# A state-space layer inside an attention phase: one generator per unit cut into a front and a back with step tables of their own

## The chip, the cores and the metric

The kernel runs on one core of a Trainium2 chip. The metric is the device time of one execution in microseconds (us), taken as the median of several executions. The engines are called PE (TensorE, the matrix multiplies; PEld is its weight load), ACT (ScalarE), DVE (VectorE), POOL (GpSimd) and SP (SyncE, which here only issues DMAs; SPq is its queue).

## The reference

One layer of a trunk with two parallel head groups, for 2048 tokens of width 1024, all in float32. The part that the change touches is the state-space mixer: 32 groups of 16 channels, each group with one diagonal complex state of 64 entries.

```python
h = rmsnorm(x, norm_mix_g)
proj = h @ w_in                      # u_ssm | q | k | v, 512 columns each
# head group A: S5 layer
bu = einsum('bsgh,gph->bsgp', u, b_bar)          # 16 inputs -> 64 complex states
_, states = associative_scan(combine, (lam_bar, bu), axis=1)
y = einsum('bsgp,ghp->bsgh', states, c_mat).real + d_skip * u
y = gelu(y.reshape(bsz, seq, 512))
y_ssm = y * sigmoid(y @ w_glu + b_glu)
# head group B: 64-frame chunks that see themselves and the 8 chunks before
y_att = chunked_attention(q, k, v, attn_rel_bias)
mixed = concat([rmsnorm(y_ssm), rmsnorm(y_att)])
x = x + mixed @ w_out
x = x + (silu(rmsnorm(x) @ w_gate) * (rmsnorm(x) @ w_up)) @ w_down
out = rmsnorm(x)
```

## The kernel before

Products of float32 accuracy are made of three passes over operands that are split into a high and a low part (names that end in h and l, or begin with hi and lo). TensorE's instructions are pinned in the order in which the program issues them; the other engines' order follows from a scheduler with those pins.

The kernel has phases: projection of the first block, the attention phase, the mixing phase (GELU, GLU, output projection), and the feed-forward network. The state-space layer is computed inside the **attention phase** (`att_phase`). That phase goes through 128 steps, one for each token block sb (4 blocks of 512 tokens), head pair pr (4), head of the pair hh (2) and query tile qp (4). In each step, in the order of `ORDER = "sptf"`, come the scores of the step (tile `sc`; VectorE adds the bias at L857, ScalarE takes the exponential at L860), the product of probabilities and values of a head that is complete, the transposes of the probabilities of two steps ago (tile `pt`; ScalarE's cast `pth` at L875, VectorE's remainder `ptl` at L876), and last the filler units.

A filler is a generator in a `Unit`: its yields are spread evenly over the steps s0 to s1, and its first piece may be taken `pre` steps ahead. Fillers are the projections of the next block (tile `pf`), queries, keys and values, and the eight units of the state-space layer, b = 0 to 7, each with four of the 32 groups (`GB` = 4). `SU` gives the steps between which each unit lies: 2, 19, 35, 49, 64, 78, 93, 107 and 122.

A unit works on chunks of eight tokens, so that the scan runs over 256 chunks (`NC`) rather than over 2048 tokens. It has these parts, in `ssm_unit`:

- loads on SyncE's queue at L564: the input `U` (eight DMAs), `Bst` (one), `Tm` (eight) and `Vm` (one), then `YL` = 8 empty sub-steps;
- the front product U times Bst into the PSUM tile `pj`, which ScalarE copies into `X` (L588, eight copies);
- the scan over the chunks on GpSimd (L602 to L614), on X in place;
- the shifted states `XG`, written from X by four DMAs on GpSimd's queue (L636), then `YX` = 9 empty sub-steps;
- the back product Tm times U plus Vm times XG into `pj`, copied by ScalarE (L646) into a tile `Y` that takes X's buffer, and stored by eight DMAs on SyncE's queue (L649) to the buffer `y` in device memory.

That makes 42 sub-steps over 13 to 17 steps. U, X, XG, Tm, Vm and Bst have one buffer each, so a unit's loads wait until the unit before has read them, and its copies into X until the unit before has stored Y.

The mixing phase opens at step `OPEN` = 119: it asks for the GLU weights (`load_wg`, raw tile `sg`, cast at L156 into `wgh` and `wgl`) and then, in `load`, for the first two blocks of y (tile `yr`, L1031). Its GELU stands at L1035 (tile `ys`), its casts into `gh` at L156, and the first GLU product `pf<-gh,wgh` follows at step 122 and later (`GSTART`). The attention's last steps run beside it.

`S["rsn"]` is an SBUF tile of 2048 columns, one per token, that holds the roots of the RMS norms. The first norm's are read when a block's input is scaled (tile `hT`, for block 1 at about steps 20 to 26, for blocks 2 and 3 later); the feed-forward norm's are written over them from the mixing phase on. Its first half, for blocks 0 and 1, is thus unused in between.

Of the kernel before, what the change touches and what calls it, by code (L numbers as in the profile page):

```python
# [16 lines left out]
P = 128  # L17
# [3 lines left out]
NG, CH, NS = 32, 16, 64  # L21
NPR = NG // 2
L = 8
NC = SEQ // L
GB, GP = 4, 2
# [20 lines left out]
SL = 1  # L46
LPH = 2
V0 = 0, 4
DB, XB = 3, 2
SU = 2, 19, 35, 49, 64, 78, 93, 107, 122  # L50
CUT = -8, -2, 2, 7, 13, 19, 24
CUTL = -8, -2, 2, 7, 13, 19, 23
ORDER = "sptf"
PINA = True
YL = 8
YX = 9
X1B = 6
TAIL = (0, 512), (512, 256), (768, 256)
MAGIC = 12582912.0
# [494 lines left out]
    return nb  # L554


def ssm_unit(k, p, psum, S, b, eng):

    nc = k.nc
    F = GB * CH  # L560
    U = k.t(p, "U", [P, GB, NC])

    def load(out, in_):
        ins = nc.sync.dma_start(out, in_)  # L564
# [5 lines left out]
    gs = slice(GB * b, GB * b + GB)  # L570
    bst = k.t(p, "Bst", [P, GB, P])
    load(bst[:].rearrange("p g m -> p (g m)"), S["bst"][b // 2][:, (b % 2) * GB * P : (b % 2 + 1) * GB * P])
    tm = k.t(p, "Tm", [P, GB, P])
    for i in range(L):
        load(tm[i * CH : (i + 1) * CH], S["kt"].rearrange("c g a m -> c g (a m)")[:, gs, P - CH * i : 2 * P - CH * i])
    vm = k.t(p, "Vm", [P, GB, P])
    load(vm[:], S["v"].rearrange("q g c n m -> (c n) (q g) m")[:, gs, CH:])
    for _ in range(YL):
        yield

    X = k.t(p, "X", [P, 2, GP, NC])
    for q in range(GP):
# [51 lines left out]
    for g2 in range(2):  # L634
        for c in range(2):
            eng.dma_start(XGv[c * NS : (c + 1) * NS, :, g2, 1:], X[g2 * NS : (g2 + 1) * NS, c, :, : NC - 1])  # L636
# [16 lines left out]
SSM_N = YL + GP + 7 + 7 + 3 + 4  + YX + GP  # L653


class Unit:
# [21 lines left out]
def att_phase(k, ident, S, aw, x0, roots):  # L678

    tc, nc, io, pfs = k.tc, k.nc, k.io, k.pfs  # L680
    with ExitStack() as cx:
# [253 lines left out]
        for sb in range(NSB):  # L935
            g0 = sb * 32
            C = CUT if sb < NSB - 1 else CUTL
            if sb > 0:
                if DB:
                    units.append(Unit(hT_unit(sb, 0, DB), 2 + DB, g0 + HTA[0], g0 + HTA[1], 2))  # L940
                units += [Unit(hT_unit(sb, DB), 2 + KT - DB, g0 + HTS[0], g0 + HTS[1], HTP), Unit(qk_unit(sb, 0), QK_N, g0 + C[0], g0 + C[1], 3, light=LIGHT)]
            units.append(Unit(v_unit(sb, 0), V_N, g0 + C[1], g0 + C[2], 2, light=LIGHT) if sb else Unit(v0, V_N, *V0, done=1))
            for gen, n, c in ((qk_unit(sb, 1), QK_N, 2), (qk_unit(sb, 2), QK_N, 3), (v_unit(sb, 1), V_N, 4), (qk_unit(sb, 3), QK_N, 5)):
                units.append(Unit(gen, n, g0 + C[c], g0 + C[c + 1], 2, light=LIGHT) if sb else Unit(gen, n + 1, C[c], C[c + 1], 4, light=LIGHT, mid=2))
        for b in range(NG // GB):
# [28 lines left out]
def mix_phase(k, S, bank):  # L974
# [3 lines left out]
    with ExitStack() as cx:  # L978
# [41 lines left out]

        yrs = [None]

        def load(sb, one=False):
            b = B()
            b.o = {}
            yt = k.t(my, "ys", [P, 4, SB], bufs=2)
            b.ys, b.g = [yt[:, f] for f in range(4)], []
            if sb % 2 == 0:
                yrs[0] = k.t(my, "yr", [P, 4, L, 128])
                for f in range(4):  # L1030
                    nc.sync.dma_start(yrs[0][:, f], S["y"][f * P : (f + 1) * P, :, sb * 64 : sb * 64 + 128])  # L1031
            yv = b.yr = yrs[0][:, :, :, (sb % 2) * 64 : (sb % 2 + 1) * 64]
            fs = [slice(0, 4)] if one else [slice(f, f + 1) for f in range(4)]
            for s in fs:
                nc.scalar.activation(yt[:, s].rearrange("p f (c j) -> p f c j", j=L), yv[:, s].rearrange("p f j c -> p f c j"), AF.Gelu_apprx_tanh)  # L1035
# [100 lines left out]
        def pre_tiles():  # L1136
            while True:
# [579 lines left out]
```

## Time and profile before

| | |
|---|---|
| median of 3 executions | 2294.59 us (2293.13 to 2301.24) |
| profiled execution | 2293.41 us, span of its trace 2291.6 us |
| mean granted clock of TensorE | 0.978 |
| TensorE busy | 2172.1 us, 95% of the span |
| VectorE, ScalarE, GpSimd busy | 1542.1, 1000.9, 359.2 us |
| the window 128 to 752 us (attention phase) | TensorE busy 551.0 of 624 us, granted clock 0.95 |
| the window 752 to 985 us (mixing phase) | TensorE busy 224.3 of 233 us, granted clock 0.98 |
| DMA | 428.34 MB moved, mean 187 GB/s |

In the profile's rows an operation reads "output<-inputs", with the line in the kernel ahead of it (L79 and L82 are the helpers that record every matmul and transpose, so products are told apart by their tiles). An "x8" behind a row counts neighbouring instructions of one kind. What stands in square brackets behind a row of the timeline is the engine's idle time ahead of it and what ended that.

### The profile page before, as it was taken

How to read it: one execution, taken by the hardware profiler on the slowest of the kernel's cores; microseconds unless marked ns; L12 is line 12 of the kernel's file. 1: busy time of each engine (PE TensorE's matmuls, PEld its weight loads, DVE VectorE, ACT ScalarE, POOL GpSimd, SP SyncE). 2: the span in 40 equal slices, each digit the busy share in tenths (PEclk: the TensorE clock that was granted, in tenths of full speed). 3: DMA queues.
4: the chain of work that ended last, by engine and by line, in shares of the span. 5: the costliest groups of instructions: out<-in, count | busy, mean ns of one | idle time of the engine just before them, and what ended most of it. 6: DMA issues, size and time to landing. Idle time of an engine off the chain costs nothing.

```text
span 2291.6 us, 30320 instructions
## 1 busy us (share of the span) xinstructions
PE 2172.1 (95%) x10632; PEld 1828.7 (80%) x10632; DVE 1542.1 (67%) x2695; ACT 1000.9 (44%) x1654; POOL 359.2 (16%) x827
## 2 busy tenths in 40 slices
PE   8987799989987899999999999999999999999997
PEld 6776688888986688878888887888888878888886
DVE  7745565555545855876776668666656477788776
ACT  6445555455546652343333335333333343354322
POOL 2246645456641000000000000000000010000000
PEclk9999999999998999999999999999999999999999
DMA  8766777766644434854564557564423295465552
GB/s 292 241 219 225 227 236 193 190 181 191 191 120 143 161 111 146 284 176 145 162 200 165 198 184 261 184 198 161 167 87 121 84 397 196 165 212 193 207 188 74
DMA packets 214872, 428.34 MB, mean 187 GB/s; under 512 B 38848, under 2 KB 61424, under 8 KB 207616
## 3 DMA queue, kind: packets, MB, share of 16 engines
q1 hardware_dynamic: 207072, 401.49, 54.2%
q0 software_dynamic: 7648, 24.92, 3.2%
q8 instruction: 83, 1.36, 0.2%
q14 instruction: 69, 0.57, 0.1%
HBM read 286.86 MB, written 129.00 MB: 181 GB/s over the span
## 4 chain that ended last, share of the span: by engine, by line
PE 73%; POOL 8%; issue 6%; DVE 4%; DMA 3%; ACT 2%; SPq 1%; DVEq 0%; POOLq 0%; ACTq 0%
PE X L79 20%; PE ps L79 17%; PE Y L79 10%; PE big L79 9%; PE pf L79 5%; PE W L79 5%; PE pj L79 3%; POOL X L605 2%; POOL st L602 1%; POOL st L603 1%; POOL X L604 1%; POOL X L614 1%; POOL fx L613 1%; PE sc L79 1%; PE pt L82 1%
## 5 line engine op out<-in xcount | busy, mean ns | idle before, releaser
L79 PE MATMUL X<-hi,c 128*128 128x512 f32 x1408 | 451.6, 391 | 7.7 <-DVE c L156 5.4
L79 PE MATMUL ps<-hd,hd 128*128 128x512 f32 (+1 forms) x1968 | 428.2, 379 | 3.2 <-DVE hd L156 2.0
L79 PEld LDWEIGHTS ps<-hd,hd 128*128 128x128 f32 x1968 | 356.4, 188 | 73.4 <-DVE hd L156 2.7
L79 PEld LDWEIGHTS X<-hi,c 128*128 128x128 f32 x1408 | 265.6, 189 | 64.0 <-DVE c L156 6.3
L79 PE MATMUL X<-lo,c 128*128 128x512 f32 x704 | 275.1, 391 | 0.0
L156 ACT CAST hd<-hd 128x1536 fp32r<-128x1536 f32 (+1 forms) x106 | 147.3, 1394 | 232.8 <-DMA hd<-hq 165.5
L79 PE MATMUL Y<-hi,c 128*128 128x512 f32 x704 | 225.1, 390 | 1.9 <-DVE u L1396 1.9
L156 DVE TENSOR_TENSOR hd<-hd 128x1536 fp32r<-128x1536 f32 (+1 forms) x106 | 174.1, 1644 | 35.0 <-ACT hd L156 34.5
L156 DVE TENSOR_TENSOR c<-S,c 128x512 fp32r<-128x512 f32 x176 | 121.0, 688 | 100.6 <-ACT c L156 100.3
L1500 POOL DMA_DIRECT2D hd<-hq x7 | 5.3, 764 | 1133.4 <-PE X L79 1121.1
L1392 ACT COPY u<-X 128x512 f32<-128x512 f32 x132 | 77.5, 588 | 201.4 <-PE X L79 201.4
L156 ACT CAST c<-S 128x512 fp32r<-128x512 f32 x176 | 109.4, 622 | 119.8 <-PE Y L79 61.6
L79 PE MATMUL big<-m,woh 128*128 128x512 f32 x512 | 161.0, 396 | 0.0
L1534 DVE TENSOR_TENSOR acc<-acc,ps 128x512 f32<-128x512 f32 x196 | 130.4, 683 | 41.6 <-PE ps L79 41.4
L79 PEld LDWEIGHTS Y<-hi,c 128*128 128x128 f32 x704 | 132.8, 189 | 30.5 <-DVE u L1396 2.8
L79 PEld LDWEIGHTS X<-lo,c 128*128 128x128 f32 x704 | 132.9, 189 | 27.7
L79 PE MATMUL pf<-hi,w 128*128 128x512 f32 x416 | 150.1, 412 | 4.0 <-ACT hi L736 4.0
L156 ACT CAST c<-raw 128x512 fp32r<-128x512 f32 x132 | 82.3, 623 | 151.4 <-PE Y L79 68.5
L79 PE MATMUL Y<-lo,c 128*128 128x512 f32 x352 | 137.3, 390 | 0.0
L876 DVE TENSOR_TENSOR ptl<-pt,pth 128x640 fp32r<-128x640 f32 (+3 forms) x152 | 98.3, 647 | 45.9 <-ACT pth L875 44.4
L860 ACT ACTIVATE s<-s,mn 128x640 f32<-128x640 f32 (+4 forms) x128 | 98.0, 765 | 58.5 <-DVE mn L857 53.6
L875 ACT CAST pth<-pt 128x640 fp32r<-128x640 f32 (+3 forms) x152 | 83.8, 551 | 87.4 <-PE pt L82 82.5
(443 smaller groups left out, 4290.3 us busy)
## 6 DMA issues: line engine op xcount, KB each, us to landing
w<-wss SPq DMA_DIRECT2D x36, 1024.0 KB, 6.3
hq<-g SPq DMA_DIRECT2D x140, 256.0 KB, 2.1
hd<-hq SPq DMA_DIRECT2D x35, 768.0 KB, 4.4
hd<-wc SPq DMA_DIRECT2D x35, 768.0 KB, 5.9
raw<-in_w_gate SPq DMA_DIRECT2D x44, 512.0 KB, 3.7
raw<-in_w_up SPq DMA_DIRECT2D x44, 512.0 KB, 4.2
wc<-px SPq DMA_DIRECT2D x66, 256.0 KB, 3.4
wss<-w SPq DMA_DIRECT2D x12, 1024.0 KB, 4.9
```

The costliest lines, as they stand in the source:

```text
L79: return self.tc.keep_in_program_order(self.tc.nc.tensor.matmul(*a, **b))
L82: return self.tc.keep_in_program_order(self.tc.nc.tensor.transpose(*a, **b))
L156: return nc.scalar.copy(hi, raw), nc.vector.tensor_tensor(lo, raw, f32(hi), op=ALU.subtract)
L602: eng.tensor_tensor(t[:, :, :, :n], src, ar, op=ALU.mult)
L603: eng.tensor_tensor(t2[:, :, :, :n], src[:, ::-1], aw, op=ALU.mult)
L604: eng.tensor_tensor(dst, dst, t[:, :, :, :n], op=ALU.add)
L605: eng.tensor_tensor(dst, dst, t2[:, :, :, :n], op=ALU.add)
L860: nc.scalar.activation(s[:, :nk], s[:, :nk], AF.Exp, bias=mn[:], scale=-1.0, accum_out=sums[sb, pr][:, hh, qp : qp + 1])
L875: nc.scalar.copy(pth[:, a:b, qp, :], pt[:, a:b, :])
L876: nc.vector.tensor_tensor(ptl[:, a:b, qp, :], pt[:, a:b, :], f32(pth[:, a:b, qp, :]), op=ALU.subtract)
L1392: nc.scalar.copy(u[:], ps[:])
L1534: V.tensor_tensor(a, a, ps[:], op=ALU.add)
```

## The change

`ssm_unit` is cut in two generators. `ssm_front` has the loads of U and Bst, the front product, the scan and the XG DMAs, in 25 sub-steps over nine steps from `SX[b]` on (4, 24, 35, 48, 61, 74, 87, 100); its first piece, the loads, is taken five steps ahead (two for units 0 and 1). `ssm_back` has the loads of Tm and Vm, six steps ahead, then the back product in two steps from `SY[b]` on (20, 36, 49, 62, 75, 88, 101, 114), and the eight stores of y. The empty sub-steps and their constants are gone.

U has a second buffer: for b = 2, 4 and 6 it lies in the first half of `S["rsn"]`; for b = 0 and the odd units it is the tile U as before. The output is no longer copied into a tile in X's buffer but over U, and stored from there, so X is free as soon as its XG transfers have read it. The mixing phase gets a `fetch`, which asks for the first two blocks of y when that phase opens, ahead of the GLU weights; before, the same DMAs were in `load(0)`, behind them.

All loads and stores stay on SyncE's queue, and the number and shapes of the matmuls, copies and GpSimd operations are the same.

```diff
-SU = 2, 19, 35, 49, 64, 78, 93, 107, 122
-YL = 8
-YX = 9
...
-def ssm_unit(k, p, psum, S, b, eng):
+def ssm_front(k, p, psum, S, b, eng):
...
-    U = k.t(p, "U", [P, GB, NC])
...
+    U = S["rsn"][:, : GB * NC].rearrange("p (g c) -> p g c", g=GB) if b and b % 2 == 0 else k.t(p, "U", [P, GB, NC])[:]
+    k.U[b] = U
     for j in range(L):
         load(U[j * CH : (j + 1) * CH].rearrange("c g (n t) -> c g n t", n=NSB), S["u"].rearrange("(c g) n j t -> c g n j t", c=CH)[:, GB * b : GB * b + GB, :, j])
...
-    for _ in range(YL):
-        yield
+    yield
...
             eng.dma_start(XGv[c * NS : (c + 1) * NS, :, g2, 1:], X[g2 * NS : (g2 + 1) * NS, c, :, : NC - 1])
-    for _ in range(YX):
-        yield
-    Y = k.t(p, "X", [P, GB, NC])
+    yield
+
+
+def ssm_back(k, p, psum, S, b):
...
+    tm = k.t(p, "Tm", [P, GB, P])
+    for i in range(L):
+        nc.sync.dma_start(tm[i * CH : (i + 1) * CH], S["kt"].rearrange("c g a m -> c g (a m)")[:, gs, P - CH * i : 2 * P - CH * i])
+    vm = k.t(p, "Vm", [P, GB, P])
+    nc.sync.dma_start(vm[:], S["v"].rearrange("q g c n m -> (c n) (q g) m")[:, gs, CH:])
+    yield
+    U, XG = k.U.pop(b), k.XG
     for q in range(GP):
...
-        nc.scalar.copy(Y[:, 2 * q : 2 * q + 2, :], ps[:])
-        if q == GP - 1:
-            for j in range(L):
-                nc.sync.dma_start(S["y"][b * F : (b + 1) * F, j, :].rearrange("(g c) t -> c g t", c=CH), Y[j * CH : (j + 1) * CH])
+        nc.scalar.copy(U[:, 2 * q : 2 * q + 2, :], ps[:])
         yield
+    for j in range(L):
+        nc.sync.dma_start(S["y"][b * F : (b + 1) * F, j, :].rearrange("(g c) t -> c g t", c=CH), U[j * CH : (j + 1) * CH])
+    yield
...
+SX = 4, 24, 35, 48, 61, 74, 87, 100
+SY = 20, 36, 49, 62, 75, 88, 101, 114
...
-            units.append(Unit(ssm_unit(k, sp, psum, S, b, k.ssm_eng), SSM_N, SU[b], SU[b + 1], light=SL))
+            units.append(Unit(ssm_front(k, sp, psum, S, b, k.ssm_eng), SSM_F, SX[b], SX[b] + 9, SX[b] - 2 if b == 0 else 2 if b == 1 else 5, light=SL))
+            units.append(Unit(ssm_back(k, sp, psum, S, b), SSM_B, SY[b], SY[b] + 2, 6, light=SL))
...
+        def fetch(sb):
+            yrs[0] = k.t(my, "yr", [P, 4, L, 128])
+            for f in range(4):
+                nc.sync.dma_start(yrs[0][:, f], S["y"][f * P : (f + 1) * P, :, sb * 64 : sb * 64 + 128])
...
-            if sb % 2 == 0:
-                yrs[0] = k.t(my, "yr", [P, 4, L, 128])
-                for f in range(4):
-                    nc.sync.dma_start(yrs[0][:, f], S["y"][f * P : (f + 1) * P, :, sb * 64 : sb * 64 + 128])
+            if sb and sb % 2 == 0:
+                fetch(sb)
...
+        fetch(0)
         load_wg()
```

Three places show how the instructions move. In the rows, the number behind a tile's name tells its instances apart.

**TensorE, unit 1's back and unit 2's front.** Before, unit 1's back product (with XG) stands at step 34 and unit 2's front product (with Bst) three steps later, behind a part of the next block's projection (pf):

```order
L79 MATMUL pf_3331<-hi2x_2647,w_3237 128x512
L79 MATMUL pj_3342<-U_2553,Tm_2564 128x256
L79 MATMUL pj_3342<-XG_2326,Vm_2573 128x256
...
L79 MATMUL pj_3348<-XG_2326,Vm_2573 128x256
L79 MATMUL sc_3362<-k_608_2803,q2h_2801 128x320
...
L79 MATMUL pf_3448<-lo_605_2797,w_3239 128x512
L79 MATMUL pf_3448<-hi_604_2796,w_3239 128x512
L79 MATMUL pj_3489<-U_3398,Bst_3407 128x256 x2
L79 MATMUL pj_3496<-U_3398,Bst_3407 128x256 x2
L79 MATMUL sc_3505<-k_611_2806,q2h_2804 128x320
```

In the new order the front of unit 2 comes first, at step 35, with its U in rsn, and unit 1's back one step later, from the tile U:

```order
L76 MATMUL pj_3387<-rsn_92,Bst_3130 128x256 x2
L76 MATMUL pj_3394<-rsn_92,Bst_3130 128x256 x2
L76 MATMUL sc_3407<-k_597_2755,q2h_2753 128x320
...
L76 MATMUL pf_3435<-hi1x_2563,w_3238 128x512
L76 MATMUL pj_3442<-U_2677,Tm_3111 128x256
L76 MATMUL pj_3442<-XG_2225,Vm_3120 128x256
...
L76 MATMUL pj_3448<-XG_2225,Vm_3120 128x256
L76 MATMUL sc_3472<-k_597_2755,q2h_2753 128x320
```

The back has moved from three steps ahead of the next unit's front to one step behind it.

**SyncE's queue between units 0 and 1.** Before, unit 0's stores (y), the store of attention's output (ya_s), and unit 1's loads stand ahead of the next block's input (xt) and of the copies that make the second head's queries (q2h, q2l):

```order
L649 DMA y_65<-X_2491 16x4x256 x8
L910 DMA ya_s_66<-ya_2278 128x512
L564 DMA U_2553<-u_64 16x16x64 x8
L564 DMA Tm_2564<-kts_78 16x4x128 x8
L564 DMA Vm_2573<-vs_71 128x4x128
L717 DMA xt_2599<-in_xt 128x512
L779 DMA q2h_2533<-q2h_2533 64x512
L780 DMA q2l_2534<-q2l_2534 64x512
L779 DMA q2h_2536<-q2h_2536 64x512
```

In the new order one row of the next block's input, the first y store, and the query copies come first, then the other stores, more input, and unit 1's loads:

```order
L722 DMA xt_2671<-in_xt 128x512
L651 DMA y_65<-U_1705 16x4x256
L707 DMA w_2623<-wss_74 128x2048
L784 DMA q2h_2512<-q2h_2512 64x512
L785 DMA q2l_2513<-q2l_2513 64x512
L784 DMA q2h_2515<-q2h_2515 64x512
L785 DMA q2l_2516<-q2l_2516 64x512
L651 DMA y_65<-U_1705 16x4x256 x7
L722 DMA raw_2675<-in_xt 128x2x512
L559 DMA Bst_2686<-bsts_70 128x512
L559 DMA U_2677<-u_64 16x16x64 x8
```

The query copies have moved ahead of seven of the stores and of unit 1's loads; unit 1's Tm and Vm stand further down, six steps ahead of its back.

**ScalarE at the hand-over to the mixing phase.** Before, the GELU (ys) follows three exponentials of scores and their casts (L875), and the second GELU comes ahead of the next exponential's table load:

```order
L860 ACTIVATE s_8266,sm_8090<-s_8266,mn_8267 128x640
L875 CAST pth_8175<-pt_8270 128x5x128
L1035 ACT_TABLE_LOAD
L1035 ACTIVATE ys_8191<-yr_8192 128x2048
L1011 ACTIVATE sq_8222<-ya_1760_8214 128x512
L156 CAST gh_1752_8198<-ys_8191 128x512
...
L1014 ACTIVATE sg_8227<-ya_1762_8216 128x512
L1035 ACTIVATE ys_8472<-yr_8192 128x2048
L1014 ACTIVATE sg_8230<-ya_1763_8217 128x512
L860 ACT_TABLE_LOAD
L860 ACTIVATE s_8290,sm_8090<-s_8290,mn_8291 128x640
```

In the new order the GELU stands right behind an exponential, ahead of the cast of the transposed probabilities (L880, the old L875), and the two GELUs have two exponentials between them:

```order
L865 ACTIVATE s_8141,sm_8105<-s_8141,mn_8142 128x640
L1045 ACT_TABLE_LOAD
L1045 ACTIVATE ys_8185<-yr_8069 128x2048
L153 CAST wgh_1709_8074<-sg_8076 128x512
L153 CAST wgh_1712_8080<-sg_8082 128x512
L904 COPY yt_8166<-pj_8149 64x512
L880 CAST pth_8169<-pt_8171 128x5x128
...
L865 ACT_TABLE_LOAD
L865 ACTIVATE s_8231,sm_8105<-s_8231,mn_8232 128x640
...
L1045 ACT_TABLE_LOAD
L1045 ACTIVATE ys_8461<-yr_8069 128x2048
```

The GELU of the first block has moved ahead of two casts and some weight casts behind it, and two table loads have come in. From the mixing phase's later products on, both programs have the same rows.

More of the change, by code (lines that the diff above doesn't have):

```diff
@@ L554, in bias_rows @@
     return nb
-def ssm_unit(k, p, psum, S, b, eng):
+def ssm_front(k, p, psum, S, b, eng):
     nc = k.nc
-    F = GB * CH
-    U = k.t(p, "U", [P, GB, NC])
     def load(out, in_):
@@ L566, in load @@
             k.tc.keep_in_program_order(ins)
+    U = S["rsn"][:, : GB * NC].rearrange("p (g c) -> p g c", g=GB) if b and b % 2 == 0 else k.t(p, "U", [P, GB, NC])[:]
+    k.U[b] = U
     for j in range(L):
         load(U[j * CH : (j + 1) * CH].rearrange("c g (n t) -> c g n t", n=NSB), S["u"].rearrange("(c g) n j t -> c g n j t", c=CH)[:, GB * b : GB * b + GB, :, j])
-    gs = slice(GB * b, GB * b + GB)
     bst = k.t(p, "Bst", [P, GB, P])
     load(bst[:].rearrange("p g m -> p (g m)"), S["bst"][b // 2][:, (b % 2) * GB * P : (b % 2 + 1) * GB * P])
[L573 to L577, printed above, removed]
-    for _ in range(YL):
-        yield
+    yield
     X = k.t(p, "X", [P, 2, GP, NC])
@@ L636, in ssm_unit @@
             eng.dma_start(XGv[c * NS : (c + 1) * NS, :, g2, 1:], X[g2 * NS : (g2 + 1) * NS, c, :, : NC - 1])
-    for _ in range(YX):
-        yield
-    Y = k.t(p, "X", [P, GB, NC])
+    yield
+def ssm_back(k, p, psum, S, b):
+    nc = k.nc
+    F = GB * CH
+    gs = slice(GB * b, GB * b + GB)
+    tm = k.t(p, "Tm", [P, GB, P])
[5 more added lines that the diff above has]
+    U, XG = k.U.pop(b), k.XG
     for q in range(GP):
@@ L645, in ssm_unit @@
             k.ta.matmul(ps[:, g2, :], vm[:, g, :], XG[:, g, :], start=False, stop=True)
-        nc.scalar.copy(Y[:, 2 * q : 2 * q + 2, :], ps[:])
-        if q == GP - 1:
-            for j in range(L):
-                nc.sync.dma_start(S["y"][b * F : (b + 1) * F, j, :].rearrange("(g c) t -> c g t", c=CH), Y[j * CH : (j + 1) * CH])
+        nc.scalar.copy(U[:, 2 * q : 2 * q + 2, :], ps[:])
         yield
-SSM_N = YL + GP + 7 + 7 + 3 + 4  + YX + GP
+    for j in range(L):
+        nc.sync.dma_start(S["y"][b * F : (b + 1) * F, j, :].rearrange("(g c) t -> c g t", c=CH), U[j * CH : (j + 1) * CH])
+    yield
+SSM_F = 1 + GP + 7 + 7 + 3 + 4 + 1
+SSM_B = 1 + GP + 1
+SX = 4, 24, 35, 48, 61, 74, 87, 100
+SY = 20, 36, 49, 62, 75, 88, 101, 114
 class Unit:
```

1 line of the change is left out of this document (added).

## The prediction

> **What bounds the kernel now.** I read the page first, then TensorE's own table of waits, then its timeline around the long waits, then the granted clock there, and last the queues of the engines that it waits for. The page's span and its first section:
>
> ```profile
> span 2291.6 us, 30320 instructions
> ...
> PE 2172.1 (95%) x10632; PEld 1828.7 (80%) x10632; DVE 1542.1 (67%) x2695; ACT 1000.9 (44%) x1654; POOL 359.2 (16%) x827
> ```
>
> TensorE is busy for 95% of the span, and the change neither adds nor removes a matmul: whatever it gains comes out of TensorE's idle time and of time at a low clock. TensorE's waits (line waited for: us in total, times, longest):
>
> ```profile
> PE pj L79 <- DMA XG<-X: 14.2, 2, 8.4
> PE pj L79 <- DMA Tm<-kts: 8.1, 5, 3.8
> PE pf L79 <- ACT gh L156: 6.8, 1, 6.8
> PE pj L79 <- issue: 1.9, 1, 1.9
> ```
>
> Three of the four are at the state-space layer's own products (tile pj). XG is the shifted state that GpSimd's scan leaves by DMA; "Tm" stands for the whole batch of loads ahead of a unit. The timeline gives their places:
>
> ```profile
> 218.44 1.19 PE L79 MATMUL pj<-XG,Vm 128*128 128x256 f32 x2 [8.45 <-DMA XG<-X]
> 499.64 1.19 PE L79 MATMUL pj<-XG,Vm 128*128 128x256 f32 x2 [5.79 <-DMA XG<-X]
> 633.02 0.68 PE L79 MATMUL pj<-XG,Vm 128*128 128x256 f32 x2 [1.95 <-issue]
> 651.25 3.75 PE L79 MATMUL pj<-U,Bst 128*128 128x256 f32 x8 [3.79 <-DMA Tm<-kts]
> ```
>
> Units 0, 4 and 6 reach their output product before XG has landed: 8.45 + 5.79 + 1.95 = 16.2 us. The loads cost 8.1 us. Behind each wait the clock is low for a while; these are windows of TensorE's granted clock (the column ahead of the last two):
>
> ```profile
> 218.00:228.00 10.00, 9.56 (x34) 7.87 (x35) 3.09 (x7) 3.36 (x8) 0.00 (x0) 0.70 0.17 28
> 500.00:510.00 10.00, 10.00 (x52) 8.90 (x52) 2.07 (x4) 3.71 (x7) 0.00 (x0) 0.81 0.30 52
> 630.00:640.00 10.00, 8.05 (x35) 6.56 (x34) 2.21 (x5) 2.33 (x5) 0.00 (x0) 0.83 0.31 61
> 650.00:660.00 10.00, 8.75 (x36) 7.75 (x37) 0.93 (x3) 4.52 (x12) 3.23 (x7) 0.66 0.66 166
> ```
>
> Busy time by the missing clock is 9.56 x 0.30 + 10 x 0.19 + 8.05 x 0.17 + 8.75 x 0.34 = 9.1 us. So what the layer's waits cost is at most 16.2 + 8.1 + 9.1 = 33.4 us.
>
> **The change part by part.** All sums are against the profiled execution, 2293.4 us (span 2291.6 and 1.8 around it), which lies 1.2 us under the median 2294.59.
>
> *1. Front and back apart (XG waits).* A back now stands 14 steps behind its front's first product (16 for unit 0, 12 for unit 1). What a front needs until XG has landed, and how fast steps go by, is in these rows: GpSimd's first scan instruction and last XG issue of units 0 and 1, the landing times of unit 1's XG, a front's eight copies, the scores of steps 24, 36 and 124, and the first and the following row of the last unit's product:
>
> ```profile
> 166.18 0.53 POOL L602 TENSOR_TENSOR st<-X,a 128x128 f32<-128x128 f32 x1 [27.21 <-ACT X L588]
> 242.91 0.49 POOL L602 TENSOR_TENSOR st<-X,a 128x128 f32<-128x128 f32 x1 [30.10 <-ACT X L588]
> 285.35 1.21 POOL L636 DMA_DIRECT2D XG<-X  x2 [0.30 <-POOL X L614]
> DMA to landing us min/median/max: 4.1/6.1/7.8
> 451.49 3.04 ACT L588 COPY X<-pj 64x256 f32<-64x256 f32 x8 [3.98 <-PE pj L79]
> 250.69 0.28 DVE L857 CUSTOM_DVE_ANT_0 s<-sc,nba 128x128 f32<-128x128 f32 x1
> 305.28 0.82 DVE L857 CUSTOM_DVE_ANT_0 s<-sc,nbb 128x640 f32<-128x640 f32 x1 [0.52 <-DMA y<-X]
> 712.33 0.82 DVE L857 CUSTOM_DVE_ANT_0 s<-sc,nbb 128x640 f32<-128x640 f32 x1 [0.96 <-PE sc L79]
> 700.70 0.60 PE L79 MATMUL pj<-U,Tm 128*128 128x256 f32 x2
> 703.97 0.50 PE L79 MATMUL sc<-k,q2h 128*128 128x320 f32 x1
> ```
>
> A step lasts (712.33 - 250.69) / 100 = 4.6 us, so 14 steps are 64 us. A front needs 3.6 us for its copies, 43.7 us of GpSimd (242.91 to 286.56, the longer kind) and 6.1 to 7.8 us to land: 53 to 55 us. Units 2 to 7 have 9 us to spare, and their waits go. Unit 1 has only 12 steps, and these are quicker than in the trace: 305.28 - 250.69 = 54.6, less a 3.1 us stall (part 4), less the 3.3 us of unit 1's own product (700.70 to 703.97 for such a one), which stood inside, plus 1 us for unit 2's front: 49.2 us, against 53.4. ScalarE has unit 2's copies one step earlier, and they need the one X buffer that the same XG transfers read; the softmax is queued behind them. I price this at 4.2 us of XG and 1.5 us for the first four copies that free the product's bank, 5.5 us; it can be 0 or 11. Unit 0's front starts its scan about 2 us sooner, since both its products now stand in step 4; the scan until XG takes 52.3 us (166.18 to 218.44), so XG is there at 216.5. Its back stands two steps later than the 209.4 at which TensorE got there, so it waits 0 to 2.3 us; I take 2. Sum: -16.2 + 5.5 + 2 = -8.7 us (0 to -16).
>
> *2. Loads ahead (U buffer, loads 5 steps early).* From unit 2 on, U and Bst are asked for five steps, 23 us, ahead of the product, into the other buffer, and Tm and Vm six steps ahead of the back. Of the 8.1 us, unit 1 may keep some: its loads start two steps ahead and now wait until unit 0's output has been read out of the same U. -8.1 + 1.5 = -6.6 us (-4 to -8). Unit 0's Tm and Vm move to the head of SyncE's queue, past the halves of the first query block; SyncE is idle there:
>
> ```profile
> 113.25 0.38 SPq L686 DMA_DIRECT2D raw<-in_w_qk  x1
> 129.45 0.49 SPq L779 DMA_DIRECT2D hi0x<-hi0x  x1
> ```
>
> Nine issues of under half a microsecond fit into 16 us, so this costs nothing; without that cover it would delay the first scores by 4 us.
>
> *3. The clock.* 9.1 us, of which the two waits left in part 1 bring back some 3.6 (two windows such as the second and third above): -5.5 us (0 to -9). [...]
>
> *4. What stood behind the layer's bursts on SyncE's queue.* At unit 1, the page's list of SyncE issues has U x8 and Tm x8 ahead of the copies that make step 24's queries, and ahead of the input of block 1; TensorE waited for both:
>
> ```profile
> 229.23 3.95 SPq L564 DMA_DIRECT2D U<-u  x8
> 233.22 3.73 SPq L564 DMA_DIRECT2D Tm<-kts  x8
> 239.93 0.54 SPq L780 DMA_DIRECT2D q2l<-q2l  x1
> 244.70 1.29 SPq L717 DMA_DIRECT2D raw<-in_xt  x2
> 247.96 0.45 PE L79 MATMUL sc<-k,q2h 128*128 128x128 f32 x1 [3.93 <-issue]
> 256.12 0.49 PE L79 MATMUL pf<-hi,w 128*128 128x512 f32 x1 [3.12 <-ACT hi L736]
> ```
>
> In the new order these copies and the first of the two input loads stand ahead of the burst, the second still behind eight y stores. Of 7.05 us I take 4.5 off (0 to 7).
>
> *5. The hand-over to the next phase.* ScalarE's and TensorE's rows there:
>
> ```profile
> 706.30 0.83 ACT L860 ACTIVATE s<-s,mn 128x640 f32<-128x640 f32 x1 [1.08 <-DVE mn L857]
> 708.37 0.69 ACT L875 CAST pth<-pt 128x640 fp32r<-128x640 f32 x1
> 715.38 0.69 ACT L875 CAST pth<-pt 128x640 fp32r<-128x640 f32 x1 [1.20 <-PE pt L82]
> 716.14 1.28 ACT L1035 ACT_TABLE_LOAD   x1
> 717.44 3.64 ACT L1035 ACTIVATE ys<-yr 128x2048 f32<-128x2048 f32 x1
> 721.50 2.16 ACT L156 CAST gh<-ys 128x512 fp32r<-128x512 f32 x4
> 722.16 0.79 PE L79 MATMUL pf<-gh,wgh 128*128 128x512 f32 x1 [6.81 <-ACT gh L156]
> ```
>
> The GELU starts as soon as its table is loaded, and that right behind the cast of 715.38: it waits for ScalarE's order, not for y. An earlier y therefore gains nothing by itself. In the new order table load and GELU stand right behind the exponential of 706.30, and with two weight casts (about 0.6 each, a quarter of the 721.50 row) push the next cast from 708.4 to 714.7; behind that stand four gh casts, two more weight casts, two squares, a table load, an exponential and two squares (2.2 + 1.2 + 1.2 + 1.3 + 1.0 + 1.2), so the cast that the last transposes ahead of the first gh product wait for ends at 723.6, and with its DVE twin and the transposes the product starts at 725.2, not 722.16: 3 us later. One more for the last unit's 3.3 us of product, which now fill no waits here: +4 us (-5 to +8). What speaks against the change at this place: the GELUs of the two blocks now have an exponential between them, which adds two table loads, 2 x 1.28 us. [...]
>
> *6. Copies side by side.* A front's eight copies now stand one step ahead of the back's two (three steps apart before). With the 3.04 us above and 1.2 for the back's, ScalarE has 4.2 us more within two steps of 9.2; a few tenths at each of seven places: +2 us (0 to 7).
>
> Y's own tile is gone and the output goes over U: no instruction more or less, 0 us.
>
> Sum: -8.7 - 6.6 - 5.5 - 4.5 + 4 + 2 = -19.3, so **2274 us**.
>
> **The rivals.**
> *A, all waits go.* XG of units 0 and 1 lands in time and the hand-over is no later: -16.2 - 8.1 - 9.1 - 7.05 = -40, 2253 us. For it: GpSimd's faster units take 5 us less. Against it: the 12 steps of unit 1.
> *B, no change.* XG's waits come back at units 0 and 1 in full (the 16.2 and their clock return), the loads go (-6.6), half of part 4 goes (-3.5), and the hand-over costs 7: 2290 us. For it: at 706.30 and 715.38 ScalarE already waits on DVE and TensorE, so the softmax chain is near.
> *C, slower: one X buffer.* ScalarE's copies of a front wait, with the softmax behind them, until the XG transfers of the front before have read X. Fronts are 13 steps apart, 60 us in the trace and about 57 without its stalls; 55 us fit. If the scan with its landing took 62 us, each of six units would block for 5 us and 1.5 for the copies: +39 - 19 = 2312 us. It decides from about 61 us on. Against it: the longest here, unit 0's, needs 52.3 + 3.6 = 56.
>
> **How the numbers follow.** Forecast 0.60 (its own range 2262 to 2286), A 0.13, B 0.18, C 0.09. The range that leaves out C and the far part of A is 2256 to 2292. About 0.5% (2283 to 2306 around the median) is what a measurement can tell from no change. Faster: nearly all of the forecast and A, 0.71; same: the forecast's upper end and most of B, 0.20; slower: C, 0.09.
>
> **What would show it.** In TensorE's waits XG and Tm fall from 14.2 and 8.1 to under 8 and 3, with what is left at units 0 and 1. Granted clock over the attention phase rises. ScalarE shows a wait for XG's transfers ahead of unit 2's copies. The first gh product waits for gh or for pt as long as before. Wrong would be: waits at units 2 to 7, a hand-over that is over 8 us later, or waits of pt for ptl that grow with what XG gave up.

## The result, and the profile after

The changed kernel takes 2277.18 us (median of 6 runs, 2275.79 to 2278.23) against 2294.14 us of the kernel before (6 runs, 2288.95 to 2301.24). The ratio is 0.9928 with a 95% interval of [0.9913, 0.9943]: 17 us, or 0.7%, faster. The forecast was 2274.0.

The page's first section after (span 2275.6 us) has TensorE's share where it was:

```profile
PE 2169.8 (95%) x10632; PEld 1828.5 (80%) x10632; DVE 1542.7 (68%) x2695; ACT 1002.5 (44%) x1656; POOL 350.1 (15%) x827
```

For all comparisons below the profiled execution is cut in two. The **stretch** goes from VectorE's first score operation to the first product in tile big; it holds everything that the change moves. The **rest** comes behind it and has the same instructions in both programs. First row and last row of the stretch, of before and then of after:

```profile
136.54 0.29 DVE L857 CUSTOM_DVE_ANT_0 s<-sc,nba 128x128 f32<-128x128 f32 x1 [2.13 <-PE sc L79]
751.33 0.48 PE L79 MATMUL big<-gh,wgh 128*128 128x512 f32 x1
```
```profile
136.96 0.29 DVE L862 CUSTOM_DVE_ANT_0 s<-sc,nba 128x128 f32<-128x128 f32 x1 [2.19 <-PE sc L76]
731.43 0.48 PE L76 MATMUL big<-gh,wgh 128*128 128x512 f32 x1
```

The stretch went from 614.8 to 594.5 us, 20.3 us shorter. The rest went from 1540.3 to 1544.2 us (span less 751.33, and less 731.43), 3.9 us longer with the same instructions; the last section shows why. Windows over the stretch of before and of after (TensorE's busy time stands right behind the length):

```profile
136.54:751.33 614.79, 548.92 (x3258) 487.06 (x3258) 342.64 (x660) 332.31 (x680) 302.10 (x712) 0.95 0.65 189
```
```profile
136.96:731.43 594.47, 544.04 (x3259) 485.96 (x3258) 343.73 (x660) 335.03 (x682) 293.14 (x712) 0.95 0.67 194
```

TensorE's idle time (length less busy time) fell from 65.87 to 50.43 us, by 15.4, and its busy time by 4.9. Of the 4.9 us the clock has 2.6: by the traces' records of the granted clock TensorE worked at half clock for 45.3 us of the stretch before and for 40.1 after. What the other 2.3 us are is not shown. In TensorE's table of waits after, the rows for XG and Tm are gone. In their place X (0.2 us before) and ks came in, and the waits for ptl and mn grew from 13.5 and 2.9 us:

```profile
PE pt L79 <- DVE ptl L881: 17.9, 8, 6.1
PE sc L76 <- DVE mn L862: 9.9, 5, 3.8
PE pj L76 <- ACT X L578: 4.3, 2, 3.1
PE pj L76 <- DMA ks<-k: 4.2, 1, 4.2
```

TensorE's timeline after gives the places of the new waits (what is waited for stands at the end):

```profile
232.70 0.30 PE L76 MATMUL sc<-k,q2h 128*128 128x128 f32 x1 [2.20 <-issue]
240.77 3.75 PE L76 MATMUL pj<-U,Bst 128*128 128x256 f32 x8 [4.20 <-DMA ks<-k]
292.06 1.09 PE L76 MATMUL pj<-U,Tm 128*128 128x256 f32 x2 [3.05 <-ACT X L578]
386.52 0.80 PE L76 MATMUL pf<-lo,w 128*128 128x512 f32 x1 [3.58 <-DVE lo L742]
406.79 0.38 PE L76 MATMUL sc<-k,q2h 128*128 128x320 f32 x1 [3.75 <-DVE mn L862]
466.11 0.43 PE L76 MATMUL sc<-k,q2h 128*128 128x320 f32 x1 [2.64 <-DVE mn L862]
537.13 1.22 PE L76 MATMUL pj<-rsn,Bst 128*128 128x256 f32 x4 [3.46 <-DVE ya L905]
```

240.77 is unit 1's front: its U may only be loaded when unit 0's output has been stored from the same tile. (The row names ks<-k, which this product does not read; it was issued right behind the eighth load of U.) 292.06 is unit 1's back behind unit 2's copies, and ScalarE's row there names the one X buffer:

```profile
290.51 3.02 ACT L578 COPY X<-pj 64x256 f32<-64x256 f32 x8 [7.73 <-DMA XG<-X]
```

The waits for mn at 406.79 (step 60) and 466.11 (step 72) come from SyncE's queue. Its rows ahead of step 60, and VectorE's score operation:

```profile
384.17 0.54 SPq L559 DMA_DIRECT2D rsn<-u  x1
396.48 0.34 SPq L756 DMA_DIRECT2D k<-ks  x1
396.86 3.38 SPq L559 DMA_DIRECT2D rsn<-u  x7
400.77 0.45 SPq L549 DMA_DIRECT2D nbb<-nbs  x1
405.81 0.83 DVE L862 CUSTOM_DVE_ANT_0 s<-sc,nbb 128x640 f32<-128x640 f32 x1 [3.28 <-DMA nbb<-nbs]
```

The queue stood still from 384.7 to 396.5 at a load of k, whose tile TensorE's scores were still reading up to 396.4. When it moved again, seven loads of unit 4's U went first, and the bias rows (nbb) that the next head's scores need came 4.3 us behind.

### The profile page after: what moved, and what is told of

Read it like the earlier page. It is cut to its first block, busy times and chain, and to the rows that moved or that the text cites. A ratio compares the mean times of both kernels' runs of the same rounds, so it can differ in the third digit from the quotient of the medians.

```text
span 2275.6 us, 30307 instructions
## 1 busy us (share of the span) xinstructions
PE 2169.8 (95%) x10632; PEld 1828.5 (80%) x10632; DVE 1542.7 (68%) x2695; ACT 1002.5 (44%) x1656; POOL 350.1 (15%) x827
## 4 chain that ended last, share of the span: by engine, by line
PE 77%; DMA 5%; DVE 5%; issue 4%; POOL 3%; ACT 2%; SPq 1%; DVEq 0%; ACTq 0%; POOLq 0%
PE X L76 20%; PE ps L76 17%; PE Y L76 10%; PE big L76 9%; PE pf L76 8%; PE W L76 5%; PE pj L76 3%; PE sc L76 2%; DMA acc<-x 2%; PE pt L79 2%; POOL X L595 1%; POOL X L594 1%; DMA lo<-hc 1%; POOL X L604 1%; POOL fx L603 1%
## 5 line engine op out<-in xcount | busy, mean ns | idle before, releaser
L880 ACT CAST pth<-pt 128x640 fp32r<-128x640 f32 (+3 forms) x152 | 83.6, 550 | 82.6 <-PE pt L79 77.6
```

The costliest lines, as they stand in the source:

```text
L880: nc.scalar.copy(pth[:, a:b, qp, :], pt[:, a:b, :])
```

## Experiments

All kernels compute the whole reference. Times are medians; the ratio is against the kernel before, run beside each; stretch and rest are of the profiled execution. Between the five sets of runs the median of the kernel before lay between 2291 and 2296 us.

| kernel | time, us | ratio, interval | stretch | rest |
|---|---|---|---|---|
| before | 2294.14 | | 614.8 | 1540.3 |
| the change | 2277.18 | 0.9928 [0.9913, 0.9943] | 594.5 | 1544.2 |
| e1_loads3 | 2275.71 | 0.9924 [0.9905, 0.9943] | 599.2 | 1539.2 |
| e2_late_fetch | 2279.23 | 0.9935 [0.9915, 0.9954] | 602.3 | 1542.0 |
| e3_unit2_later | 2269.18 | 0.9897 [0.9880, 0.9913] | 596.2 | 1534.8 |
| e4_fronts11 | 2292.40 | 1.0001 [0.9987, 1.0015] | 619.3 | 1541.9 |
| e5_old_spaced | 2289.35 | 0.9985 [0.9967, 1.0003] | 612.3 | 1541.9 |
| e6_unit0_back18 | 2287.97 | 0.9972 [0.9955, 0.9989] | 612.5 | 1537.7 |
| e7_aligned | 2281.25 | 0.9960 [0.9944, 0.9976] | 608.3 | 1539.2 |
| e8_loads_on_act | 2309.03 | 1.0078 [1.0057, 1.0099] | 631.5 | 1540.6 |
| e9_spread_loads | 2281.03 | 0.9942 [0.9922, 0.9962] | 600.8 | 1541.8 |
| e10_unit1_later | 2273.13 | 0.9904 [0.9882, 0.9927] | 593.8 | 1538.4 |
| e11_bias_first | 2271.94 | 0.9888 [0.9870, 0.9906] | 591.4 | 1541.8 |
| e12_bias_first_loads3 | 2264.42 | 0.9866 [0.9847, 0.9884] | 588.4 | 1538.8 |

The rest, the same instructions in all fourteen, spreads over 9.4 us. A difference in time of a few us between two kernels is therefore only put down to an edit where the stretch shows it too. The stretch has its own weakness: it comes from one execution, which in e2, e4, e5 and e7 was the slowest of its kernel, 2.8, 6.0, 4.5 and 4.1 us above the median.

### Is unit 0's distance what pays?

```diff
-SY = 20, 36, 49, 62, 75, 88, 101, 114
+SY = 18, 36, 49, 62, 75, 88, 101, 114
```

> The changed kernel with unit 0's back at step 18, where it was before, in place of 20; nothing else moves. Theory W: XG has not landed there, TensorE waits about as long as two steps last less what it had to spare (it reached step 20 at 215.3 and did not wait; step 18 is reached at 204.5): some 8 us, with one or two clock windows 3 to 4 us more, of which unit 1's loads, now asked for earlier, give back up to 4: 2277 + 6 = 2283 (2281 to 2288). Rival (the gain at unit 0 is the two loads hoisted to the head of SyncE's queue and its earlier scan, and the distance is not needed): 2276 to 2279.

It took 2287.97 us, and its stretch 612.5. With two steps at one unit, 10.8 us of the 17 gained are gone by the medians, 10.1 by the ratios, and 18.0 of 20.3 in the profiled stretch. The ten runs lie further apart than those of the change: seven between 2285.7 and 2291.1 us, and three at 2277.2, 2277.5 and 2280.6; why is not shown. TensorE's timeline has the wait for XG back, and a longer one at unit 1's front:

```profile
213.04 1.19 PE L76 MATMUL pj<-XG,Vm 128*128 128x256 f32 x2 [6.67 <-DMA XG<-X]
251.55 3.75 PE L76 MATMUL pj<-U,Bst 128*128 128x256 f32 x8 [6.45 <-DMA ks<-k]
```

By step 20 it was 10.2 us behind the change, by step 92 14.9, by the end of the stretch 17.2 (start times of the steps compared). Of the 18.0 us by which the stretch is longer, TensorE's idle time has 9.6 and its busy time 8.5, nearly all of it clock: it worked at half clock for 56.4 us, against 40.1. Theory W holds, at the upper end of its range; the rival, that the hoisted loads do it, falls.

### Could the old structure have had it by its table?

```diff
-SU = 2, 19, 35, 49, 64, 78, 93, 107, 122
+SU = 2, 21, 36, 50, 64, 79, 93, 108, 122
```

> The kernel before with its own table alone changed: SU = 2, 21, 36, 50, 64, 79, 93, 108, 122, so that unit 0 has 19 steps rather than 17 and units 4 and 6 have 15 rather than 14; one U buffer, loads at a unit's start, output in X's buffer, y fetched late. Theory W (the gain is the waits for XG of units 0, 4 and 6 and what lies behind unit 0's burst, and the second buffer is only the way to get the distance): unit 0's 8.45 goes, units 4 and 6 lose 5.79 and 1.95 less what is left of them, some of it comes back at units 3 and 5, with the clock about 10 us: 2283, half of the change's gain or more. Theory B (the second buffer and the loads ahead are what gives the time): 2289 to 2294, with the waits for XG at other units and those for Tm as before.

It took 2289.35 us; the interval of its ratio reaches 1. The waits for XG of units 0, 4 and 6 are gone, and two others have come:

```profile
364.89 1.19 PE L79 MATMUL pj<-XG,Vm 128*128 128x256 f32 x2 [6.23 <-DMA XG<-X]
697.30 1.19 PE L79 MATMUL pj<-XG,Vm 128*128 128x256 f32 x2 [3.86 <-issue]
242.03 3.48 PE L79 MATMUL pj<-U,Bst 128*128 128x256 f32 x8 [8.54 <-DMA Tm<-kts]
```

They stand at unit 7, which has 14 steps in place of 15, and at unit 2, which has 14 as before but whose back TensorE reached 42 us behind its front rather than 48. Unit 1's load burst cost 8.54. With one unit at a time the steps are all given out: what one unit gets another lacks. The outcome is theory B's for this table; that no other table of the old structure would do is not shown.

### Does the one X buffer decide below 55 us?

```diff
+SX = 4, 24, 35, 46, 57, 68, 79, 90
+SY = 20, 36, 47, 58, 69, 80, 91, 102
```

> The changed kernel with fronts 11 steps apart from unit 1 on (24, 35, 46, 57, 68, 79, 90) and backs one step behind the next front. Theory X (the one X buffer decides below about 55 us between fronts): 11 steps are 49 to 51 us, so ScalarE waits 3 to 6 us for XG ahead of the copies of each of units 3 to 7, TensorE about 3 us each: 2277 + 5 x 3 = 2290 (2284 to 2300). Rival (GpSimd's faster units need only 45 us and the wait at unit 2 was unit 1's alone): 2275 to 2281 with no such waits.

2292.40 us is what theory X asked for, and yet it fell: ScalarE waited for XG ahead of unit 2's copies only (7.64 us), as in the change, and at none of units 3 to 7. From unit 3's copies to unit 4's it was only 51.3 us, and still no wait for XG. The stretch was 24.8 us longer (in the slowest of ten runs) for another reason, which TensorE's table of waits names:

```profile
PE pf L76 <- DMA w<-wss: 19.2, 5, 11.1
PE sc L76 <- DVE mn L862: 10.4, 5, 7.0
```

The weights arrived late, with 19.2 us of waits where the change had none; the waits for mn are about those of the change (9.9). Ahead of the longest, 11.1 us, the rows of SyncE's queue have three loads of Tm, the Vm and eight of U in front of the weights: closer units put more on the queue. A total that comes out right does not show its cause.

### Is it the bursts on SyncE's queue that took part of the gain back?

Four kernels move the bursts. The first asks for U later:

```diff
-SX[b] - 2 if b == 0 else 2 if b == 1 else 5
+SX[b] - 2 if b == 0 else 2 if b == 1 else 3
```

> The changed kernel, but the loads of U and Bst for units 2 to 7 are asked for three steps ahead of the front product, not five; in SyncE's order the bias rows (nbb, nba) of steps 60 and 72 then stand ahead of the eight U loads of units 4 and 5, not behind them. Theory Q (the bursts on SyncE's queue are what the change gave back): VectorE's waits for nbb and nba (3.28 and 1.99) and TensorE's waits for mn behind them (3.75 and 2.64) go, and no product waits for U, since three steps are 14 us: 2277 - 6.4 = about 2270. Theory S (the softmax chain has no slack there, so the waits come back at the next step as waits for ptl or mn): 2275 to 2279. Theory P (five steps are needed): waits for U return, up to the 8.1 us of before: 2285.

The time was 2275.71, in theory S's range and not told apart from the change; the stretch is 4.7 us longer. The waits for mn fell from 9.9 to 4.4 us (VectorE still waited 2.09 for nba at step 72), and TensorE waited instead for w (3.5 in two), at unit 4's front (1.99) and at unit 1's back (4.30). The second aligns everything with the bias rows:

```diff
+SX = 4, 24, 37, 49, 61, 73, 85, 97
+SY = 20, 38, 50, 62, 74, 86, 98, 110
-SY[b], SY[b] + 2, 6
+SY[b], SY[b] + 2, 3 if b else 6
```

> The changed kernel with fronts 12 steps apart from unit 2 on, at steps 37, 49, 61, 73, 85, 97 and each back one step behind the next front, the loads of U three steps ahead and those of Tm three steps ahead, so that every burst on SyncE's queue is asked for just behind the bias rows (asked for at every fourth step), and no front falls on the step in which a head's product needs the same bank. Theory Q: the waits for nbb and nba (6.4 of TensorE), the wait of unit 6's front for ya (3.46) and that for X (4.3) all go: 2277 - 14 - 2 for the clock = 2261 to 2264. Theory S (something else is next, the waits come back elsewhere): 2268 to 2275, about as with unit 2 alone moved. Theory X: at 12 steps XG's transfers hold X and ScalarE waits: over 2280.

2281.25 us is worse than every theory but X, and X is not the cause: ScalarE waits for XG's transfers nowhere. VectorE's waits for nba and nbb and unit 6's for ya went, and waits for the weights, 8.7 us in four, took their place.

The third hands the loads of units 2 to 7 to ScalarE:

```diff
-ins = nc.sync.dma_start(out, in_)
+ins = (nc.scalar if b > 1 else nc.sync).dma_start(out, in_)
```

> The changed kernel with the loads of U, Bst, Tm and Vm of units 2 to 7 issued by ScalarE rather than by SyncE; the same DMAs, sizes and steps. Theory Q (what the bursts cost is their place on SyncE's queue): the waits of VectorE for nbb, nba and in_xt go, and TensorE's 3.75 + 2.64 + 1.59 with them; ScalarE pays 18 issues of about half a microsecond for each unit within the softmax chain, 9 us for each of six units, of which it has room for most (busy 44%): 2277 - 8 + 0 to 10 = 2269 to 2279. Rival D (the cost is the transfers themselves, which share the DMA engines): the same waits for nbb and nba stay, 2277 to 2287.

It took 2309.03 us. Theory Q was right on the queue for the bias rows: VectorE waits for nbb and nba nowhere and the waits for mn fell to 2.3 us, so it is the place on the queue and not the transfers. VectorE's waits for in_xt, which it also expected to go, stayed (8.9 us, 7.3 in the change). Theory Q was wrong on the price: TensorE's waits for ptl grew from 17.9 to 57.7 us, so the softmax chain, which has ScalarE in it, had no room for 18 issues per unit.

The fourth starts from e3 and spreads the loads, two DMAs a step over five steps (`ssm_loads` and `ssm_taps` are the load loops of front and back as generators of their own):

```diff
+units.append(Unit(ssm_loads(k, sp, S, b), 5, SX[b] - 7, SX[b] - 2, light=SL))
+units.append(Unit(ssm_taps(k, sp, S, b), 5, SY[b] - 7, SY[b] - 2, light=SL))
```

> The kernel with unit 2's front two steps later (2269 in the earlier run), and the loads of U and Bst, and of Tm and Vm, of units 2 to 7 spread: two DMAs a step over five steps, from seven to two steps ahead of their product, in place of eight or nine at once. Theory Q (what stands behind a burst of eight to eighteen issues on SyncE's queue pays, be it bias rows, weights or input): no more than two to four issues, 2 us, stand ahead of anything, so TensorE's waits for mn behind nbb and nba (3.73 + 2.43) and for lo (1.66) go, and none for w<-wss come in their place: 2269 - 7 = 2262. Theory S (the waits only change places): 2267 to 2273.

2281.03 us is outside both ranges, and theory Q as it stood falls, with 16.1 us of waits for mn. SyncE's rows ahead of step 60 show why spreading does not help:

```profile
388.16 0.40 SPq L776 DMA_DIRECT2D k<-ks  x1
395.59 0.34 SPq L776 DMA_DIRECT2D k<-ks  x1
...
399.31 0.45 SPq L549 DMA_DIRECT2D nbb<-nbs  x1
```

The second load of k blocks the queue for 7 us; whatever was asked for meanwhile gathers behind it, spread or not, and the bias rows come last. So the last two kernels ask for the bias rows at a head's first tile, ahead of that load:

```diff
-            if qp == 2 and (sb, h) < (NSB - 1, H - 1):
+            if qp == 0 and (sb, h) < (NSB - 1, H - 1):
```

> The kernel with unit 2's front two steps later (2269), and the bias rows of the next head asked for at a head's first query tile rather than its third, when their buffer has just come free; the state-space loads are as in the change. In SyncE's order the rows of steps 60 and 72 then stand ahead of the loads of k that blocked the queue for 8 to 12 us, and of the bursts. Theory K (what TensorE paid at steps 60 and 72 is the place of the bias rows behind a blocked queue and what had gathered there): its waits for mn at these two steps (3.73 + 2.43) go and VectorE shows none for nbb and nba there; with the clock 2269 - 7 = 2262. Theory S (the queue is the limit: what is asked earlier pushes something else back, weights, input or the queries): 2267 to 2273, with waits for w or q2h in their place.

> The same with the loads of U and Bst of units 2 to 7 three steps ahead rather than five. Theory K: the bias rows are out of the way in either case, so 2261 to 2264 as without it. Theory S: with the loads alone three steps ahead the change gained 1.5 us, within noise, and got waits for w and for U's product in the place of those for the bias rows: 2267 to 2273 again.

In both the waits for mn at steps 60 and 72 are gone, as theory K says: over the stretch mn fell from 14.0 us in e3 to 3.2 and 2.1. But waits for w came in, 7.0 and 5.6 us where e3 had 0.3, as theory S says. In all, TensorE's idle time in the stretch is 1.2 us under e3's in e11 and 6.4 in e12, and the stretch 4.8 and 7.8. So e11 has more of theory S and e12 more of theory K; what makes the two differ is not shown. The times are 2271.94 and 2264.42; e11's rest was 7.0 us longer than e3's. The second is the fastest kernel of this study by its median, 0.9866 [0.9847, 0.9884] of the time before; the interval of e3 still touches it. Its waits over the stretch:

```profile
PE pf L76 <- DMA w<-wss: 5.6, 4, 3.2
PE sc L76 <- DVE mn L862: 2.1, 3, 1.1
```

### The early places: units 1 and 2

```diff
+SX = 4, 24, 37, 48, 61, 74, 87, 100
+SY = 20, 38, 49, 62, 75, 88, 101, 114
```

> The changed kernel with the front of unit 2 at step 37 and the back of unit 1 at step 38, each two steps later. Theory X (one X buffer: ScalarE stood 7.73 us for unit 1's XG transfers ahead of unit 2's copies, and TensorE 3.05 us for the bank): both waits go, 2277 - 3 - 1 for the clock = 2273. Rival (the wait only moves: unit 3's front is now two steps nearer, 11 steps behind unit 2's, and ScalarE waits there): 2276 to 2279, with a wait for XG ahead of unit 3's copies.

ScalarE's 7.73 us and TensorE's 3.05 went, and the time was 2269.18. But the stretch is 1.7 us longer than in the change: two waits for mn came in.

```profile
287.85 0.38 PE L76 MATMUL sc<-k,q2h 128*128 128x320 f32 x1 [2.49 <-DVE mn L862]
326.05 0.38 PE L76 MATMUL sc<-k,q2h 128*128 128x320 f32 x1 [2.34 <-DVE mn L862]
```

So in the profile nothing was gained, as the rival says, but not by its mechanism: ScalarE waits for XG's transfers nowhere, ahead of unit 3's copies neither. The 8 us lie in the rest (1534.8 against 1544.2). Whether the edit has any part in that stays open. One step later for units 1 and 2 (25, 38; backs 39, 50; unit 3 at 49):

> The kernel with unit 2's front two steps later, and the fronts of units 1 and 2 and the back of unit 1 one step later still (25, 38, 39; unit 3 at 49, unit 2's back at 50). TensorE waited 4.6 us at unit 1's front for loads of U that may only start when unit 0's output has been stored from the same tile. If that wait is fixed by the stores' landing, one step later takes up to 4.6 us off: 2269 - 4 = 2265. Rival (the stores and loads move with what stands ahead of them on SyncE's queue, or unit 3's front, now 11 steps behind unit 2's, waits for XG): 2268 to 2274.

2273.13 us, in the rival's range; the stretch is 593.8, 2.4 us under e3's. Unit 1's front still waits 2.78 us, and ScalarE's copies hold a product of probabilities for 2.21 at unit 3: in the trace partly each.

### The hand-over

```diff
-        fetch(0)
         load_wg()
...
-            if sb and sb % 2 == 0:
+            if sb % 2 == 0:
                 fetch(sb)
```

> The changed kernel with the first two blocks of y asked for where they were before, behind the GLU weights (no fetch at the opening of the mixing phase). Step 5 of the prediction (the early GELU costs 4 us at the hand-over): 2273. Theory H (the two orders of ScalarE cost TensorE the same: 15.0 us of waits between step 120 and the first product of the GLU in tile big, 14.7 before): 2276 to 2279, with the waits back at gh in place of ptl. Theory F (the early fetch is a gain of its own, as the 1.8 us by which the hand-over is shorter in the trace may say): 2279 to 2281.

2279.23 us, theory F by its figure, though the intervals of this kernel and of the change overlap. The stretch of the profiled run, the slowest of four, is 7.8 us longer than the change's; from step 120's scores to the first product in big it took 58.7 us, against 51.2. The wait for the last casts is one long one, since the GELU now waits for y itself (2.58 us ahead of its table load) with the casts behind it:

```profile
704.06 1.30 PE L79 MATMUL pt<-ident,s 128*128 128x128 f32 x5 [12.11 <-DVE ptl L881]
```

## Why the prediction was right, and where its steps were not

The total was right to 3.2 us. The stretch is 20.3 us shorter, forecast 19.3; the rest took 3.9 back in the profile. The steps, in the trace of the change, where the hand-over is the part of the stretch from VectorE's score operation of step 120 on (698.39 before, 680.27 after):

| step | forecast | measured | how |
|---|---|---|---|
| 1 XG's waits | -8.7 | -11.9 | 16.2 gone, 3.05 + 1.2 came at units 1 and 4 for X's copies |
| 2 loads | -6.6 | -3.9 | 8.1 gone, 4.2 came at unit 1's front |
| 3 clock | -5.5 | -5.4 | ahead of the hand-over, work at half clock fell from 40.2 to 29.4 us; half of that |
| 4 behind the bursts at unit 1 | -4.5 | -4.9 | 7.05 gone, 2.20 left |
| 5 hand-over | +4 | +1.5 | its length went from 52.9 to 51.2, but 3.3 us of unit 7's product stood inside it before |
| 6 copies side by side, all else | +2 | +4.3 | what is left to -20.3 |

The sum came nearer than its terms: step 1 gained 3.2 us more than forecast and the hand-over cost 2.5 less, the loads gained 2.7 less and step 6 cost 2.3 more. That these nearly cancel is luck.

**Step 1** had the right places and the right mechanism (units 2 to 7 without a wait; ScalarE at unit 2's copies behind unit 1's XG). Unit 0, priced at 2 us, waited for nothing: TensorE reached the product at 218.0. That the distance decides at unit 0 is shown by e6. (The 3.6 us for a front's copies stands in none of the rows shown, which have 3.04.)

**Step 2** had unit 1's dependence on the stores of unit 0 but sized it at 1.5 us; it was 4.2.

**Step 3** came out at its figure, and the prediction was right to count the wait of 1.95 us too, whose window had 0.83. One-us windows of the same place in the trace before (the number ahead of the last two is the granted clock):

```profile
633.00:634.00 1.00, 0.98 (x4) 0.78 0.02 4
634.00:635.00 1.00, 1.00 (x4) 0.50 0.00 0
635.00:636.00 1.00, 1.00 (x3) 0.50 0.00 0
636.00:637.00 1.00, 1.00 (x4) 0.52 0.00 0
637.00:638.00 1.00, 1.00 (x7) 1.00 0.00 0
```

The clock is whole or half here, and half for 0.44 + 1 + 1 + 0.96 = 3.4 us; over 10 us that is a mean of 0.83. At the longer waits (8.45, 5.79 and 3.79 us) the records of the granted clock have it at half from 213.71 to 223.95, from 497.02 to 503.85 and from 650.62 to 657.45 us, and TensorE worked in these for 5.5, 4.2 and 6.2 us. With the 3.4 above that is 19.3 us at half clock, a loss of 9.7, near the prediction's 9.1.

**Step 5** had the right sign and was too large. ScalarE's GELU did move ahead of the casts, and the transposes waited for them as forecast:

```profile
695.44 1.30 PE L79 MATMUL pt<-ident,s 128*128 128x128 f32 x5 [6.14 <-DVE ptl L881]
703.56 1.30 PE L79 MATMUL pt<-ident,s 128*128 128x128 f32 x5 [5.75 <-DVE ptl L881]
```

But the step counted the casts' delay against the old 6.81 us for gh only. The other waits of the old order (1.92 and 1.75 for ptl, 2.31 for sq) went too, and the first gh product came 24.2 us behind step 120's scores, against 23.8 before. TensorE's windows over the hand-over, before and after:

```profile
698.39:751.33 52.94, 37.74 (x206) 0.87 0.41 129
```
```profile
680.27:731.43 51.16, 36.39 (x191) 0.80 0.38 123
```

The idle time is nearly the same, 15.2 and 14.8 us. The length fell by 1.8 us only because unit 7's back product (700.70 to 703.97, 16 matmuls) has moved out to step 114; without it the hand-over is 1.5 us longer, at a lower granted clock (0.87 to 0.80). The prediction's sign of being wrong, waits of pt for ptl that grow, shows here only (3.7 to 13.1 us); ahead of the hand-over they fell, from 9.8 to 4.9. In the new structure a late fetch of y makes the hand-over still longer in the trace (e2), which the times alone do not tell.

**Step 6** is the term that was too small. The sum took waits off one burst on SyncE's queue (step 4) and had none for what the moved bursts would now stand ahead of: 3.75 and 2.64 us for bias rows at steps 60 and 72. e11 shows these two to go when the bias rows come first, with waits for w in their place. Two more that it did not have are 3.46 us for ya at unit 6's front and 3.58 for lo (last section). Against them waits went that no step had forecast, the largest 3.20 us for ptl at 171.23 and 2.23 for k at 396.54 in the trace before.

**Rival C** (one X buffer, slower) happened once, at unit 2, and did not spread even at 11 steps (e4). Its sum, +39 and -19.3 on 2293.4, gives 2313, not 2312.

## What to carry to other kernels

When a pipeline is cut in two so that its halves overlap, look for the one place where the distance was shortest: here two steps at the first unit carried about 10 of 17 us. Loads that were asked for earlier took 8.1 us of waits of their own away here (4.2 us came back at unit 1) and put 3.75 and 2.64 us on the bias rows behind them on the same queue, so go along the queue past every point where it blocks and list what is due there; short, urgent loads ahead of the blocking one are worth a try (e12), with an eye on what then comes late. Compare the part that an edit can reach and the part that it can't separately, since the second moved by up to 9 us without any edit.

## What the runs showed of the hardware

**The granted clock.** In its records, in the traces of before and of the change, the level is 1 or one half, and each trace has 15 whole stretches at half clock, 3.4 to 13.7 us long before and 3.4 to 17.1 in the change. Behind the same instructions around 778 us (two groups of eight products of one column, with 0.26 us of idle time between them in the change), nothing runs at half clock in e3 (1.00 from 776 to 783 us), and in the change a stretch of 3.4 us does. Of the change, and then of e3, in one-us windows of TensorE:

```profile
777.00:778.00 1.00, 0.94 (x9) 1.00 0.00 0
778.00:779.00 1.00, 0.80 (x7) 1.00 0.41 66
...
780.00:781.00 1.00, 1.00 (x5) 0.67 0.89 340
781.00:782.00 1.00, 1.00 (x4) 0.50 0.77 295
782.00:783.00 1.00, 1.00 (x4) 0.50 0.00 0
783.00:784.00 1.00, 1.00 (x4) 0.63 0.00 0
```
```profile
781.00:782.00 1.00, 1.00 (x6) 1.00 0.04 12
```

The change ran (0.33 + 0.50 + 0.50 + 0.37) = 1.7 us of work's worth slower there. What decides whether the clock falls behind such a place is not shown. Half clock makes up most of what the rest differs by. TensorE worked at half clock in the rest for 15.9 us before, 23.4 in the change and 7.2 in e3: half of the differences is 3.8 of the 3.9 us by which the rest became longer, and 8.1 of the 9.4 between the change and e3. In all fourteen traces TensorE's idle time in the rest lies between 34.0 and 36.8 us, and its busy time, with the same instructions, between 1499.8 (e3) and 1507.4 us (the change).

**VectorE beside GpSimd.** In the change the scaling of a block's input (one input tile times the norm's roots) takes 1.69 us each where GpSimd runs its 434-element carries, and 0.70 at 389.07, where GpSimd is idle; the wait of 3.58 us for lo at 386.52 lies right behind the slow ones:

```profile
381.65 3.37 DVE L740 SCALAR_TENSOR_TENSOR raw<-raw,g_mix,rsn 128x512 f32<-128x512 f32 x2
389.07 1.40 DVE L740 SCALAR_TENSOR_TENSOR raw<-raw,g_mix,rsn 128x512 f32<-128x512 f32 x2
```
```profile
383.40 1.07 POOL L603 TENSOR_TENSOR fx<-X,a 128x434 f32<-128x434 f32 x1
```

In the traces of before and of the change the 21 of these operations in the attention phase that overlap none of GpSimd's tensor operations last 0.73 to 0.75 us one by one; the six that lie for more than half of their time beside the 434-element carries last 0.88 to 1.75, five of them over 1.5.
